# Seven-product tiles begin with a sum's product; the first block's product is copied from bank to bank and another accumulates onto it

## The chip, the core and the metric

The kernel runs on one core of one Trainium2 chip. The metric is the device time of one execution in microseconds (us); lower is better. A core has five engines that run side by side, each through its own instructions in order: TensorE (PE in the profile; its weight loads are PEld), VectorE (DVE), ScalarE (ACT), GpSimd (POOL) and SyncE (SP). They wait for each other by semaphores. Matrix products are written to PSUM, eight banks of 512 fp32 values in each of 128 partitions; everything else lies in SBUF.

## What is computed

One inference step of a small decoder of two layers, for 512 prompt tokens and 8 sample tokens together (520 columns), width 1024. Each layer is x += 0.5·SwiGLU(rms(x)), then a token mixer, then another 0.5·SwiGLU. So there are four SwiGLU blocks, and they are most of the work:

```python
def _swiglu(x, wg, wu, wd):
    return (jax.nn.silu(x @ wg) * (x @ wu)) @ wd      # 1024 -> 2816 -> 1024

for l in range(DEPTH):                                # DEPTH = 2
    x = x + 0.5 * _swiglu(_rmsnorm(x, norm_g[l, 0]), ...)
    x = x + mixer(_rmsnorm(x, norm_g[l, 1]))          # pooling in layer 0, attention in layer 1
    x = x + 0.5 * _swiglu(_rmsnorm(x, norm_g[l, 2]), ...)
```

Everything is fp32 to the reader. The kernel holds x transposed: a tile is 128 features by 520 tokens.

## The kernel before

**Products.** An fp32 matrix is held as a high and a low half (`xh`, `xl`; weights `wh`, `wl`), and a product is three passes: high·high, low·high, high·low. The halves of a weight piece of 128x512 are made on the chip: ACT rounds the raw piece to `wh` (L287), DVE subtracts to get `wl` (L288). Each piece so costs ACT one instruction and DVE one, and `_split` runs five pieces ahead of the product that uses them; `wh` and `wl` have six buffers each.

**Seven-product tiles.** A 2x2 block product needs eight block products; Strassen's scheme in Winograd's form needs seven, and more additions. Most tiles of the SwiGLU blocks are done so. For the up side (`strassen_tile`, 77 tiles) the two rows of the block matrix are the gate and the up weights of 128 hidden features, its two columns the two halves of the input features, and the token columns fall in two halves of 260. For the down side (`strassen_down`, 8 calls of 4 tiles, 32 tiles) the rows are two output tiles. The seven products are named by their weight piece and their moving side: A11·B11, S1·T1, S2·T2, A12·B21, S4·B22, S3·T3 and A22·T4. A11, A12, A22 are raw blocks; S1 is loaded by two DMAs that add up (`S` in the profile); S3 is a DMA that adds a block onto another; S2 (L221) and S4 (L227) are DVE additions in place on the raw piece. A product is 12 matmuls of 260 columns (L652; 4 slices of the contraction by 3 passes).

**Banks.** PSUM is handed out in pairs of banks, four pairs in all. A tile takes one bank `a` and a pair `c`. Before the change the up tile ran so: A11·B11 into `a`, copied by ACT to the first half of `sa` (L798); S1·T1 into the second bank of `c`, copied to `sb` (L803); then `finish()`, the last product A22·T4 of the tile before; S2·T2 onto `a`, copied to the second half of `sa` (L806); A12·B21 into the first bank of `c`; S4·B22 onto its second. DVE adds `sa` and both banks of `c` to `g` (L810, 520 columns), multiplies by `R`, the reciprocal norm of the tokens (L813), and ACT makes the Silu `t` (L814). S3·T3 goes onto `a`, DVE adds that to `sb` (L816) and multiplies by one half of `t` (L819), and the tile's last product A22·T4 onto `a` is multiplied by the other half (L821). The hidden tile `g` is then split into halves for the down side (L379, L380; and on the first two of a block's three parts the sums T1 to T4 of the down side are formed from a pair of such tiles by DVE, L709 to L729). The down tile is the same with L835, L837, L843 (copies), L850, L851 (add, multiply by `R`), L852, L854, L859 to L862. The first seven-product tile of each block (`early=True`, 4 in all) has its own order.

**What sets the order.** The program is recorded in this order, and a scheduler then orders the instructions of each engine; it may move a product's first matmuls ahead of another's. Weight pieces are listed in the order of the products (`sums`, `woven`): A11, S1, then A22 of the tile before, S2, A12, S4, S3. The ACT copies stand in ACT's one queue between the `wh` splits, so a copy comes after every split that the scheduler put ahead of it.

**Stages by time.** The SwiGLU blocks run at about 8 to 340, 380 to 710, 720 to 1050 and 1200 to 1500 us. Each is three parts: eight up tiles and a seven-product down side, the same again, then six up tiles and a plain down side.

Of the kernel before, what the change touches and what calls it, by code (L numbers as in the profile page):

```python
# [11 lines left out]
F32 = mybir.dt.float32  # L12
# [6 lines left out]
P = 128  # L19
# [120 lines left out]
class Weights:  # L140
# [99 lines left out]
    def sums(self, ch, again, first=False):  # L240

        v = self.combos(ch, again)
        head, rest = (("A11", "A12"), ("S4", "S1", "S2", "S3")) if first else (("A11", "S1"), ("S2", "A12", "S4", "S3"))
        for name in head:
            self.piece(ch, v[name])
        self.last()
        for name in rest:
            self.piece(ch, v[name])
        self.late = (ch, v["A22"])

    def woven(self, tiles):

        put = lambda i, *names: [self.piece(tiles[i][0], tiles[i][1][n]) for n in names]
        self.slow.add(tiles[1][0])
        put(0, "A11", "S1")
        self.last()
        put(1, "A11", "S1")
        put(0, "S2", "A12", "S4", "S3")
        put(1, "S2")
        put(0, "A22")  # L260
        put(1, "A12", "S4", "S3")
        for i in range(2, len(tiles)):
            put(i, "A11", "S1")
            put(i - 1, "A22")
            put(i, "S2", "A12", "S4", "S3")
        self.late = (tiles[-1][0], tiles[-1][1]["A22"])
# [58 lines left out]
def yoco_step(ctx, tc, ins, outs):  # L325
# [208 lines left out]
    def hcols(t, hf):  # L534
        return t[:, hf * H : (hf + 1) * H]


    def halves(t):
        return t.rearrange("p (h b a) -> p h b a", h=2, b=2)
# [5 lines left out]
    def back(z):  # L545

        return z.rearrange("p (b a) -> p b a", b=2)
# [9 lines left out]
    def out(bank):  # L557

        return bank[:, :H].rearrange("p (a b) -> p b a", b=2)
# [221 lines left out]
    def finish():  # L781
        if unfinished:
            unfinished.pop()()

    def strassen_tile(tmp, xx, tt, hs, early=False):

        B = lambda src, ks, hf: [tuple(hcols(z, hf) for z in src[k]) for k in ks]
        lo, up = range(4), range(4, 8)  # L790
        g = tmp.tile([P, TOK], F32, tag="g", name="g")
        t = tmp.tile([P, TOK], F32, tag="t", name="t")
        sa = tmp.tile([P, TOK], F32, tag="sa", name="sa")
        sb = tmp.tile([P, H], F32, tag="sb", name="sb", bufs=2)
        both, c = duo(), duo()
        a, b = both[:, 0, :], both[:, 1, :] if early else c[:, 1, :]
        product(B(xx, lo, 0), a)
        S.copy(back(hcols(sa, 0)), out(a))  # L798
        if early:
            product(B(xx, up, 0), c[:, 0, :])  # L800
            product(B(xx, up, 1), c[:, 1, :])
        product(B(tt, lo, 0), b)
        S.copy(back(sb), out(b))  # L803
        finish()
        product(B(tt, lo, 1), a, True)
        S.copy(back(hcols(sa, 1)), out(a))  # L806
        if not early:
            product(B(xx, up, 0), c[:, 0, :])
            product(B(xx, up, 1), c[:, 1, :], True)
        V.tensor_tensor(halves(g), halves(sa), outs(c), op=ALU.add)  # L810
        if early:
            V.tensor_tensor(hcols(g, 1), hcols(g, 1), sb, op=ALU.add)
        V.tensor_tensor(g, g, R, op=ALU.mult)  # L813
        S.activation(t, g, AF.Silu)  # L814
        product(B(tt, up, 0), a, True)
        V.tensor_tensor(back(sb), back(sb), out(a), op=ALU.add)  # L816

        def rest():
            V.tensor_tensor(hcols(g, 1), sb, hcols(t, 1), op=ALU.mult)  # L819
            product(B(tt, up, 1), a, True)  # L820
            V.tensor_tensor(back(hcols(g, 0)), out(a), back(hcols(t, 0)), op=ALU.mult)  # L821
            hidden(g, hs)

        unfinished.append(rest)

    def strassen_down(tmp, hs):
# [2 lines left out]

        def head(i):  # L830
            a, c = duo()[:, 0, :], duo()
            sa = tmp.tile([P, TOK], F32, tag="sa", name="sa")
            sb = tmp.tile([P, H], F32, tag="sb", name="sb", bufs=2)
            product(b["B11"], a)
            S.copy(back(hcols(sa, 0)), out(a))  # L835
            product(b["T1"], c[:, 1, :])
            S.copy(back(sb), out(c[:, 1, :]))  # L837
            st[i] = a, c, sa, sb

        def second(i):  # L840
            a, c, sa, sb = st[i]
            product(b["T2"], a, True)
            S.copy(back(hcols(sa, 1)), out(a))  # L843

        def third(i):
            a, c, sa, sb = st[i]
            product(b["B21"], c[:, 0, :])
            product(b["B22"], c[:, 1, :], True)
            u = tmp.tile([P, TOK], F32, tag="u", name="u", bufs=nu[0])
            V.tensor_tensor(halves(u), halves(sa), outs(c), op=ALU.add)  # L850
            V.tensor_tensor(u, u, R, op=ALU.mult)  # L851
            V.scalar_tensor_tensor(x[2 * i], u, -0.5, x[2 * i], op0=ALU.mult, op1=ALU.add)  # L852
            product(b["T3"], a, True)
            V.tensor_tensor(back(sb), back(sb), out(a), op=ALU.add)  # L854
# [1269 lines left out]
```

## Time and profile before

| | |
|---|---|
| median of 3 runs | 1534.68 us (1531.17 to 1536.09) |
| the profiled execution | 1533.06 us; its span, first to last instruction, 1531.3 us |
| mean granted TensorE clock | 0.998 |
| ACT busy | 968.8 us (63%) |
| POOL busy | 309.6 us (20%) |
| HBM | 147 GB/s over the span |

The profile is one execution. A group of instructions is a line of the kernel with an engine, an operation and operands; "mean ns of one" is its duration as recorded. Durations of following instructions overlap at their ends: 128x260 matmuls are recorded with 276 ns each, but start about 111 ns apart, and a DVE instruction of 128x520 is recorded with some 695 ns and the next starts about 0.61 us after it. So what an instruction takes from its engine is read from starts, and a busy share near 100% hides short waits. In a timeline row, what stands in brackets is the idle time before the instruction and what ended it.

### The profile page before, as it was taken

Reading aid. Unit: us, or ns where it says so; the run is one execution under the profiler, and the core shown is the slowest. Engines: PE = TensorE matmul, PEld = TensorE weight load, DVE = VectorE, ACT = ScalarE, POOL = GpSimd, SP = SyncE. Lnnn points to the kernel's source line nnn. Section 1 sums busy time; section 2 is a strip of 40 time slices with the busy share of each in tenths; the row PEclk is TensorE's granted clock in tenths of the full one; section 3 lists DMA queues with packets and bytes.
Section 4 is the critical chain, followed back from the end, with each engine's and each line's share of the span. In section 5 each row is a group of like instructions: output and inputs, shape, how many; then the busy total and the mean of one; then the engine's idle time right before and its main releaser. Section 6 shows DMA issues by size and latency. Waiting matters only on the chain. (4 is left out here: it accounts for less than half of the span.)

```text
span 1531.3 us, 35129 instructions
## 1 busy us (share of the span) xinstructions
PE 1507.3 (98%) x13338; PEld 1490.9 (97%) x13338; DVE 1407.0 (92%) x2799; ACT 968.8 (63%) x2030; POOL 309.6 (20%) x348
## 2 busy tenths in 40 slices
PE   9999999999999999999999999999999999999997
PEld 9999999999999999999999999999999999999997
DVE  6999999979999999989899999987887999999976
ACT  6765665657665665656665665655886765665555
POOL 1122222101122222100322221201561122222200
PEclk9999999999999999999999999999999999999999
DMA  9699889753688999845888998853434589988941
GB/s 244 125 192 199 188 190 203 179 173 119 139 195 183 196 193 193 179 127 131 202 191 188 198 196 184 185 173 87 88 69 99 124 180 191 197 191 189 205 130 57
DMA packets 420037, 255.43 MB, mean 167 GB/s; under 512 B 13182, under 2 KB 400246, under 8 KB 419828
## 3 DMA queue, kind: packets, MB, share of 16 engines
q1 hardware_dynamic: 339918, 187.56, 44.5%
q0 software_dynamic: 76192, 60.53, 28.2%
q10 hardware_dynamic: 3758, 5.09, 1.1%
q8 instruction: 105, 1.72, 0.5%
q14 instruction: 64, 0.52, 0.1%
HBM read 218.59 MB, written 6.11 MB: 147 GB/s over the span
## 5 line engine op out<-in xcount | busy, mean ns | idle before, releaser
L287 ACT ACTIVATE wh<-raw 128x512 fp32r<-128x512 f32 (+1 forms) x770 | 445.7, 616 | 242.6 <-DVE raw L221 79.5
L288 DVE TENSOR_TENSOR wl<-raw,wh 128x512 fp32r<-128x512 f32 (+1 forms) x770 | 501.5, 677 | 37.7 <-ACT wh L287 34.0
L652 PE MATMUL ps<-th,wh 128*128 128x260 f32 x1232 | 339.1, 276 | 0.6 <-ACT sb L803 0.4
L652 PE MATMUL ps<-th,wl 128*128 128x260 f32 x1232 | 337.7, 276 | 0.5 <-DVE wl L288 0.5
L652 PE MATMUL ps<-tl,wh 128*128 128x260 f32 x1232 | 338.1, 275 | 0.0
L652 PE MATMUL ps<-xh,wh 128*128 128x260 f32 x908 | 249.2, 276 | 1.2 <-ACT wh L287 0.9
L652 PE MATMUL ps<-xh,wl 128*128 128x260 f32 x908 | 248.7, 276 | 0.5 <-DVE wl L288 0.4
L652 PE MATMUL ps<-xl,wh 128*128 128x260 f32 x908 | 248.5, 276 | 0.0
L652 PEld LDWEIGHTS ps<-th,wh 128*128 128x128 f32 x1232 | 234.4, 190 | 2.0 <-ACT wh L287 0.9
L652 PEld LDWEIGHTS ps<-tl,wh 128*128 128x128 f32 x1232 | 234.5, 190 | 0.0
L652 PEld LDWEIGHTS ps<-th,wl 128*128 128x128 f32 x1232 | 233.6, 190 | 0.7 <-DVE wl L288 0.7
L398 POOL DMA_DIRECT2D S<-in_ffn_w_up_dram x77 | 102.1, 1326 | 419.4 <-DMA S<-in_ffn_w_up_dram 181.2
L652 PE MATMUL ps<-hh,wh 128*128 128x260 f32 x656 | 180.3, 278 | 3.5 <-ACT wh L287 1.7
L652 PE MATMUL ps<-hl,wh 128*128 128x260 f32 x656 | 179.4, 276 | 0.9 <-DVE hl L380 0.9
L652 PE MATMUL ps<-hh,wl 128*128 128x260 f32 x656 | 178.5, 275 | 0.0
L214 POOL DMA_DIRECT2D raw<-raw x109 | 96.1, 882 | 405.1 <-DVE wl L288 143.9
L652 PEld LDWEIGHTS ps<-xh,wh 128*128 128x128 f32 x908 | 172.4, 190 | 2.2 <-ACT wh L287 1.5
L652 PEld LDWEIGHTS ps<-xh,wl 128*128 128x128 f32 x908 | 172.2, 190 | 1.0 <-DVE wl L288 1.0
L652 PEld LDWEIGHTS ps<-xl,wh 128*128 128x128 f32 x908 | 172.5, 190 | 0.1
L652 PEld LDWEIGHTS ps<-hh,wh 128*128 128x128 f32 x656 | 124.2, 190 | 5.5 <-ACT wh L287 2.3
L652 PEld LDWEIGHTS ps<-hl,wh 128*128 128x128 f32 x656 | 124.4, 190 | 1.6 <-DVE hl L380 1.6
L652 PEld LDWEIGHTS ps<-hh,wl 128*128 128x128 f32 x656 | 124.1, 190 | 0.0
(370 smaller groups left out, 3609.5 us busy)
## 6 DMA issues: line engine op xcount, KB each, us to landing
raw<-in_ffn_w_gate_dram SPq DMA_DIRECT2D x87, 512.0 KB, 5.2
raw<-in_ffn_w_up_dram SPq DMA_DIRECT2D x87, 512.0 KB, 6.4
raw<-in_ffn_w_down_dram SPq DMA_DIRECT2D x128, 256.0 KB, 4.8
raw<-raw POOLq DMA_DIRECT2D x109, 256.0 KB, 4.2
S<-in_ffn_w_up_dram SPq DMA_DIRECT2D x77, 256.0 KB, 4.5
S<-in_ffn_w_up_dram POOLq DMA_DIRECT2D x77, 256.0 KB, 5.5
raw<-in_ffn_w_down_dram SPq DMA_DIRECT2D x16, 768.0 KB, 4.5
S<-in_ffn_w_down_dram SPq DMA_DIRECT2D x32, 256.0 KB, 3.1
```

Of the source, the lines that this page charges most:

```text
L214: G.dma_start(blk(raw, 2, 1), blk(raw, 1, 1), accum_op=ALU.add)
L287: pin(nc.scalar.activation(dh, src, AF.Copy))
L288: pin(nc.vector.tensor_tensor(dl, src, dh.bitcast(F32), op=ALU.subtract))
L398: return [ld(lambda t: t, a), lambda t: nc.gpsimd.dma_start(t, b, accum_op=ALU.add)]
L652: T.matmul(bank[:, :H], a[:, kk, :], two(b), start=(not more and kk == 0 and i == 0), stop=(kk == 3 and i == 2), skip_group_check=more,)
```

## The change

The seven-product tiles that aren't `early`, on the up and the down side, begin with S1·T1 and then do A11·B11; the weight pieces are listed in that order. The copy of A11·B11 goes from bank `a` into the first bank of `c` instead of into `sa`, as the whole bank's 260 columns in their order; A12·B21 then accumulates onto it (`more=True`). Only the copy of `a` after S2·T2 still goes to `sa`, which needs 260 columns. DVE adds that copy to the second bank of `c`, in place in PSUM (260 columns), and multiplies both banks by `R` in one instruction of 520 columns that reads PSUM. The number of products, matmuls, copies, splits and DMAs is the same.

```diff
     def sums(self, ch, again, first=False):
-        head, rest = (("A11", "A12"), ("S4", "S1", "S2", "S3")) if first else (("A11", "S1"), ("S2", "A12", "S4", "S3"))
+        head, rest = (("A11", "A12"), ("S4", "S1", "S2", "S3")) if first else (("S1", "A11"), ("S2", "A12", "S4", "S3"))
...
     def woven(self, tiles):
-        put(0, "A11", "S1")
+        put(0, "S1", "A11")
...
         for i in range(2, len(tiles)):
-            put(i, "A11", "S1")
+            put(i, "S1", "A11")
...
     def strassen_tile(tmp, xx, tt, hs, early=False):
-        product(B(xx, lo, 0), a)
-        S.copy(back(hcols(sa, 0)), out(a))
         if early:
+            product(B(xx, lo, 0), a)
+            S.copy(back(hcols(sa, 0)), out(a))
             product(B(xx, up, 0), c[:, 0, :])
             product(B(xx, up, 1), c[:, 1, :])
         product(B(tt, lo, 0), b)
         S.copy(back(sb), out(b))
+        if not early:
+            product(B(xx, lo, 0), a)
+            S.copy(c[:, 0, :H], a[:, :H])
         finish()
         product(B(tt, lo, 1), a, True)
-        S.copy(back(hcols(sa, 1)), out(a))
-        if not early:
-            product(B(xx, up, 0), c[:, 0, :])
+        if early:
+            S.copy(back(hcols(sa, 1)), out(a))
+            V.tensor_tensor(halves(g), halves(sa), outs(c), op=ALU.add)
+            V.tensor_tensor(hcols(g, 1), hcols(g, 1), sb, op=ALU.add)
+            V.tensor_tensor(g, g, R, op=ALU.mult)
+        else:
+            S.copy(hcols(sa, 1), a[:, :H])
+            product(B(xx, up, 0), c[:, 0, :], True)
             product(B(xx, up, 1), c[:, 1, :], True)
-        V.tensor_tensor(halves(g), halves(sa), outs(c), op=ALU.add)
-        if early:
-            V.tensor_tensor(hcols(g, 1), hcols(g, 1), sb, op=ALU.add)
-        V.tensor_tensor(g, g, R, op=ALU.mult)
+            V.tensor_tensor(c[:, 1, :H], hcols(sa, 1), c[:, 1, :H], op=ALU.add)
+            V.tensor_tensor(halves(g), outs(c), halves(R), op=ALU.mult)
         S.activation(t, g, AF.Silu)
...
     def strassen_down(tmp, hs):
         def head(i):
-            product(b["B11"], a)
-            S.copy(back(hcols(sa, 0)), out(a))
             product(b["T1"], c[:, 1, :])
             S.copy(back(sb), out(c[:, 1, :]))
+            product(b["B11"], a)
+            S.copy(c[:, 0, :H], a[:, :H])
         def second(i):
             product(b["T2"], a, True)
-            S.copy(back(hcols(sa, 1)), out(a))
+            S.copy(sa, a[:, :H])
         def third(i):
-            product(b["B21"], c[:, 0, :])
+            product(b["B21"], c[:, 0, :], True)
             product(b["B22"], c[:, 1, :], True)
-            V.tensor_tensor(halves(u), halves(sa), outs(c), op=ALU.add)
-            V.tensor_tensor(u, u, R, op=ALU.mult)
+            V.tensor_tensor(c[:, 1, :H], sa, c[:, 1, :H], op=ALU.add)
+            V.tensor_tensor(halves(u), outs(c), halves(R), op=ALU.mult)
```

The scheduler makes another order of it. Three places show what it moved; line numbers are those of each kernel, and the numbers in the names of raw pieces and banks are the same in both.

**ACT, a regular up tile** (the third part of a block; `ps_14278` is its bank `a`, `ps_14279` the second bank's pair `c`, `raw_13964` its weights, `raw_14101` and `S` those of the next tile). Before:

```order
L803 COPY sb<-ps_14279 128x260 [waits PE_49]
L287 ACTIVATE wh<-raw_13964 128x512 [waits DVE_49,Activation_49]
L287 ACTIVATE wh<-raw_13964 128x512 [waits DMAHW0_49,DMASW0_49]
L287 ACTIVATE wh<-raw_14101 128x512 [waits DMAHW2_49,Activation_49]
L287 ACTIVATE wh<-S 128x512 [waits DMASW1_49,PE_49,Activation_49]
L806 COPY sa<-ps_14278 128x260 [waits PE_49]
```

And now:

```order
L803 COPY sb<-ps_14279 128x260 [waits PE_49]
L287 ACTIVATE wh<-raw_13964 128x512 [waits DVE_49,Activation_49]
L287 ACTIVATE wh<-raw_13964 128x512 [waits DMAHW0_49,DMASW0_49,Activation_49]
L287 ACTIVATE wh<-S 128x512 [waits DMASW1_49,PE_49,Activation_49]
L806 COPY ps_14279<-ps_14278 128x260 [waits PE_49,Activation_49]
L287 ACTIVATE wh<-raw_14101 128x512 [waits DMAHW2_49,PE_49]
```

The split that waits for DVE is that of S4. Before, the copy of A11·B11 (L798) stood ahead of the first row; now it is the fifth row, behind the splits of S4, S3 and the next tile's S1, the last of which also waits for PE.

**PE, the third tile of a down side** (third block, second part; `ps_14000` is its bank `a`, `ps_13711` and `ps_13783` are the banks `a` of the first and second tile). Before, where S2·T2 (`ps_14000<-xh`) begins:

```order
L652 MATMUL ps_13711<-ph,wl 128x260
L652 MATMUL ps_13711<-ph,wh 128x260
L652 MATMUL ps_13711<-pl,wh 128x260
L652 MATMUL ps_13711<-ph,wl 128x260
L652 MATMUL ps_14000<-xh,wh 128x260
L652 MATMUL ps_14000<-xl,wh 128x260
```

And now:

```order
L652 MATMUL ps_14000<-hl,wh 128x260
L652 MATMUL ps_14000<-hh,wl 128x260
L652 MATMUL ps_13783<-ph,wh 128x260
L652 MATMUL ps_13783<-pl,wh 128x260
L652 MATMUL ps_13783<-ph,wl 128x260
L652 MATMUL ps_14138<-xh,wh 128x260
L652 MATMUL ps_14138<-xl,wh 128x260
L652 MATMUL ps_14000<-xh,wh 128x260
L652 MATMUL ps_14000<-xl,wh 128x260
```

Before, the twelve matmuls of a whole other product (`ps_13711<-ph`) stood between the end of A11·B11 (`ps_14000<-hh,wl`) and S2·T2, and the product S1·T1 behind them. Now five matmuls stand between.

**PE, the start of the same down side** (`ps_13571` is bank `a` of the last up tile, whose last product ends in the first row; `ps_13711`, `ps_13712` are `a` and `c` of the first down tile, `ps_13783`, `ps_13784` of the second). Before, from the ninth matmul of S2·T2 on, then A12·B21's first, then the second tile's S1·T1:

```order
L652 MATMUL ps_13711<-xh,wl 128x260
L652 MATMUL ps_13712<-xh,wh 128x260
L652 MATMUL ps_13784<-xh,wh 128x260
L652 MATMUL ps_13784<-xl,wh 128x260
L652 MATMUL ps_13784<-xh,wl 128x260
```

And now, from near the end of the first nine matmuls of A12·B21:

```order
L652 MATMUL ps_13712<-xl,wh 128x260
L652 MATMUL ps_13712<-xh,wl 128x260
L652 MATMUL ps_13783<-hh,wh 128x260
L652 MATMUL ps_13783<-hl,wh 128x260
L652 MATMUL ps_13783<-hh,wl 128x260
```

S1·T1 of the second tile now stands ahead of the last up tile's last product, and A11·B11 of the second tile (`ps_13783<-hh`) takes the place behind eighteen matmuls of the first down tile. The orders of SP's and POOL's DMAs are the same in both kernels, row by row.

More of the change, by code (lines that the diff above doesn't have):

```diff
@@ L254, in woven @@
         self.slow.add(tiles[1][0])
-        put(0, "A11", "S1")
+        put(0, "S1", "A11")
         self.last()
-        put(1, "A11", "S1")
+        put(1, "S1", "A11")
         put(0, "S2", "A12", "S4", "S3")
@@ L831, in head @@
             a, c = duo()[:, 0, :], duo()
-            sa = tmp.tile([P, TOK], F32, tag="sa", name="sa")
+            sa = tmp.tile([P, TOK], F32, tag="sa", name="sa")[:, :H]
             sb = tmp.tile([P, H], F32, tag="sb", name="sb", bufs=2)
-            product(b["B11"], a)
-            S.copy(back(hcols(sa, 0)), out(a))
             product(b["T1"], c[:, 1, :])
             S.copy(back(sb), out(c[:, 1, :]))
+            product(b["B11"], a)
+            S.copy(c[:, 0, :H], a[:, :H])
             st[i] = a, c, sa, sb
```

## The prediction, made before the changed kernel was run

> **What bounds the kernel.** I read the page's table of engines first, then stretches of time, then PE's waits.
>
> ```profile
> PE 1507.3 (98%) x13338; PEld 1490.9 (97%) x13338; DVE 1407.0 (92%) x2799; ACT 968.8 (63%) x2030; POOL 309.6 (20%) x348
> ```
>
> PE is the bound, and DVE stands close behind. How much PE has left is read from counts, since its busy share hides short waits. The next view gives four stretches with nearly all seven-product tiles, and one that is full (columns: stretch, then busy us and instructions of PE, PEld, DVE, ACT, POOL, then clock and DMA):
>
> ```profile
> 60.00:300.00 240.00, 238.20 (x2109) 236.20 (x2107) 233.94 (x436) 147.77 (x304) 52.48 (x48) 1.00 0.91 194
> 410.00:600.00 190.00, 188.19 (x1661) 186.47 (x1661) 186.35 (x349) 117.56 (x242) 41.50 (x38) 1.00 0.87 186
> 740.00:950.00 210.00, 208.55 (x1847) 206.95 (x1847) 203.18 (x380) 129.79 (x266) 47.36 (x45) 1.00 0.87 186
> 1215.00:1430.00 215.00, 212.21 (x1875) 210.14 (x1875) 210.37 (x396) 132.69 (x272) 46.98 (x44) 1.00 0.87 185
> 600.00:700.00 100.00, 100.00 (x898) 100.00 (x897) 90.79 (x160) 61.85 (x119) 10.94 (x10) 1.00 0.69 166
> ```
>
> The full stretch has 898 matmuls in 100 us, 0.1114 us each, at full clock. The four others have 7492 in 855 us, which would take 834.3 us. So 20.7 us of PE's time is lost there, 1.3% of the run: no edit that leaves the matmuls alone can win more. DVE is busy 833.85 of the 855 us, 97.5%: in these stretches it is nearly a second bound.
>
> Which waits are they? The waits of the seven-product matmuls' line (us, times):
>
> ```profile
> its engine sat idle before it (us, times) until:
>   ACT wh L287: 2.6, 3
>   DVE wl L288: 1.0, 2
>   DVE hl L380: 0.9, 2
>   DVE g L821: 0.8, 3
>   ACT sa L843: 0.7, 3
>   ACT hh L379: 0.5, 1
>   ACT sb L803: 0.4, 1
>   DVE g L810: 0.4, 1
>   ACT sa L835: 0.3, 1
> ```
>
> That is 7.6 us in 17 waits. Each costs more than its row says, as starts show, here where a down side begins in the fourth block:
>
> ```profile
> 1276.98 0.28 PE L652 MATMUL ps<-hh,wh 128*128 128x260 f32 x1
> 1277.53 0.38 PE L652 MATMUL ps<-hh,wh 128*128 128x260 f32 x1 [0.28 <-DVE g L821]
> 1277.75 0.28 PE L652 MATMUL ps<-hl,wh 128*128 128x260 f32 x1
> ...
> 1279.09 0.28 PE L652 MATMUL ps<-hh,wl 128*128 128x260 f32 x1
> 1280.23 0.38 PE L652 MATMUL ps<-hh,wh 128*128 128x260 f32 x1 [0.87 <-ACT wh L287]
> ```
>
> From 1276.98 to 1277.53 is 0.55 us, 0.44 more than the usual 0.11, where the row says 0.28; and the next start comes after 0.22, another 0.11. So a wait costs its row and 0.27 us: 7.6 + 17·0.27 = 12.2 us. The rest of the 20.7 us is waits too short for a row.
>
> **The second wait of that piece** is DVE's doing, through ACT:
>
> ```profile
> 1277.51 0.64 ACT L379 ACTIVATE hh<-g 128x520 fp32r<-128x520 f32 x1 [0.86 <-DVE g L821]
> 1278.51 1.67 ACT L287 ACTIVATE wh<-raw 128x512 fp32r<-128x512 f32 x3 [0.36 <-DVE raw L227]
> 1280.09 0.35 ACT L837 COPY sb<-ps 128x260 f32<-128x260 f32 x1
> ```
>
> ACT waited 0.86 us for the last up tile's multiply on DVE (L821), then for S4's addition (L227), and then made three splits, the third of which PE waited for. An ACT split takes (1280.09 − 1278.51)/3 = 0.53 us.
>
> **What the change takes from DVE.** Groups by shape, then starts:
>
> ```profile
> L813 DVE TENSOR_TENSOR g<-g,R 128x520 f32<-128x520 f32 x77 | 53.6, 696 | 0.0
> L810 DVE TENSOR_TENSOR g<-sa,ps 128x520 f32<-128x520 f32 x77 | 53.3, 692 | 1.1 <-PE ps L652 0.8
> L821 DVE TENSOR_TENSOR g<-ps,t 128x260 f32<-128x260 f32 x77 | 32.6, 424 | 6.6 <-PE ps L652 6.5
> L930 DVE TENSOR_TENSOR u<-ps,R 128x520 f32<-128x520 f32 x29 | 20.1, 696 | 6.4 <-PE ps L624 6.4
> L720 DVE TENSOR_TENSOR t<-g 128x260 f32<-128x260 f32 x32 | 13.7, 427 | 0.4
> ```
>
> ```profile
> 1346.59 0.43 DVE L819 TENSOR_TENSOR g<-sb,t 128x260 f32<-128x260 f32 x1
> 1346.93 0.43 DVE L821 TENSOR_TENSOR g<-ps,t 128x260 f32<-128x260 f32 x1
> 1347.27 0.69 DVE L288 TENSOR_TENSOR wl<-raw,wh 128x512 fp32r<-128x512 f32 x1
> 1347.87 0.69 DVE L810 TENSOR_TENSOR g<-sa,ps 128x520 f32<-128x520 f32 x1
> 1348.47 1.29 DVE L288 TENSOR_TENSOR wl<-raw,wh 128x512 fp32r<-128x512 f32 x2
> ```
>
> A tile loses an addition of 520 (692 ns) and a multiply (696), and gets an addition of 260 (424, as L821) and a multiply that reads PSUM (696, as L930): 0.268 us less, and the same from starts (0.60 against 0.34). With 73 up tiles and 32 down tiles that is 105·0.268 = 28.1 us of DVE: its share of the four stretches falls to 94.2%. No row has DVE or ACT writing PSUM. For DVE's addition the ends are 424 and 692 ns, so the relief lies between 28 us and nothing; I take 424, the row of the same width with a PSUM operand. For ACT's copy to a bank I take the 0.36 us of its copies to SBUF (the L837 row), between nothing and one split's 0.53.
>
> The Trainium skill ("Perfetto Trace Analysis", Optimizing Scalar/DVE Operations) speaks against this: it gives DVE a fixed cost of some 60 ns an instruction on SBUF and 125 on PSUM. By it, an estimate: the 260-wide addition and the multiply would both pay the higher cost where now one of two does, 65 ns a tile, and the relief would be 21 us. The rows above do not bear it out for reads: L821 reads PSUM and L720 does not, and they take 424 and 427 ns.
>
> Relief that PE doesn't wait for is worth nothing, so I count waits. By the order shown, at the start of a down side the second tile's S1·T1 no longer stands behind the last up tile's multiply (3 waits on L821), A11·B11 of the second tile fills PE while ACT makes the splits (3 on `wh`), and 28 instead of 14 matmuls lie between S2·T2 and S3·T3 of the first tile, which hides its copy (3 on L843). These nine cost 2.6 + 0.8 + 0.7 + 9·0.27 = 6.5 us. Of the other eight (3.5 + 8·0.27 = 5.7 us) I let a third go with DVE's backlog: 1.9 us. **Gain 8.4 us**; ends 1.6 (the copy waits alone, 0.7 + 3·0.27) and 12.2.
>
> **What it adds: a nearer wait.** S2·T2 may not start before the copy of A11·B11 has read `a`. Between them lay two products; now it is one, or less. Behind the copy in ACT's queue stand the splits that follow, and behind S2·T2 all of PE. When can the copy start?
>
> ```profile
> 1349.69 0.28 PE L652 MATMUL ps<-xh,wl 128*128 128x260 f32 x1
> 1350.00 0.38 ACT L798 COPY sa<-ps 128x260 f32<-128x260 f32 x1 [1.75 <-PE ps L652]
> ```
>
> 0.31 us after the product's last matmul starts. But ahead of it now stands the split of the next S1, which waits until PE has read A11's buffer: 0.31 + 0.53 + 0.36 = 1.20 us after that start. In most tiles 12 to 16 matmuls lie between, so S2·T2 is due at 13·0.111 = 1.45 us or later: covered, with 0.25 to 0.6 us to spare, and each 0.1 us that ACT is later than that costs up to 95·0.1 us. In the third tile of seven down sides, and in three early up tiles, only 2 to 5 matmuls lie between; with five, PE is ready at 6·0.111 = 0.67 us and waits 0.53. The split needs only the eleventh matmul, so up to 0.11 us less: I take 0.45. **Ten such tiles cost 4.5 us**; ends 0, if ACT finds the split done, and 10, if one more split (0.53) is ahead.
>
> The S1 piece is wanted one product (1.34 us) earlier. Its loads keep their places in SP's and POOL's queues. Now ACT waits for them little:
>
> ```profile
> ACT wh L287 <- DMA S<-in_ffn_w_down_dram: 2.5, 5, 1.0
> ```
>
> I cost it at nothing, because pieces are split five products ahead of use; without that cover it would be 1.34 us more at these five, 6.7 us.
>
> **Sum.** 1533.06 (the profiled execution, span and 1.8 us around it) − 8.4 + 4.5 = 1529.2 us. The median of the runs lies 1.6 us higher, so on its scale 1530.8; I say **1530**.
>
> **Rivals.**
>
> *ACT comes late to the copy in many tiles (slower).* The first of the splits ahead of the copy is that of S4, which waits for DVE's addition L227:
>
> ```profile
> ACT wh L287 <- DVE raw L227: 50.4, 52, 2.9
> ```
>
> That is 0.97 us in each of 52 waits. Before, PE didn't feel it, because pieces are five ahead; now the copy stands behind. From the end of S1·T1 to S2·T2 are 26 matmuls, 2.9 us, and three splits and the copy take 1.95: if the split of S4 begins more than 0.9 us after S1·T1 ends, PE waits. If DVE were as late as now, 52 tiles would pay 0.97 less the spare (some 0.36) less the relief of a tile (0.27), 0.34 us: 17.7 us, **1547**. For it speaks DVE's share of 97.5%; against it that DVE, 28 us lighter, can catch up, and that a wait of PE gives it more time, so that the lateness isn't paid in each tile anew.
>
> *The relief is hidden anyway.* The waits at a down side's start may be the length of the last tile's chain (multiply, split, subtract), not a backlog. Then only the copy waits go: 1533.06 − 1.6 + 4.5 = **1536**. For it: PE is full in the middle of the parts. Against it: the order puts other matmuls there.
>
> *All named waits go and none come*: 1533.06 − 12.2 = **1521**. It needs ACT at the ten near tiles in time.
>
> **How the numbers follow.** The forecast has 0.50, late copies 0.20, hidden 0.18, all go 0.12. About 0.3% (4.6 us) is what a measurement here tells from no change, so faster means under 1530.1: the forecast lies at that edge and, since its gain has more room than its cost, gives 0.30 to faster, 0.18 to the same and 0.02 to slower. With 0.12 from all-go, faster is 0.42; with 0.18 from hidden, the same is 0.36; with the late copies, slower is 0.22. The range goes from 1519, below all-go, to 1545, which takes in both ends of the ten tiles' cost and half of the late copies.
>
> **What would show it.** DVE's busy time near 1379 us with the addition near 424 ns and the multiply near 696; the copy to a bank near 0.36 us; no wait of PE on L821's successor at three starts of down sides; new waits of PE on the copy to a bank, some 0.2 to 0.3 us by their rows, in ten tiles. The forecast is wrong if PE's row for that copy is tens of waits long, if DVE's addition takes near 692 ns, or if 7492 matmuls fill the same 855 us as before.

## The result, and the profile after

The changed kernel takes 1538.26 us (median of 12 runs, 1534.63 to 1541.59), the kernel before 1532.24 us beside it (12 runs, 1530.12 to 1536.09). The ratio is 1.0037, with a 95% interval of 1.0026 to 1.0048: some 6 us slower, where 2 us less was forecast. The profiled execution took 1536.96 us, 3.9 us more than that of before.

The engines' line of the page of the changed kernel:

```profile
PE 1506.1 (98%) x13338; PEld 1491.1 (97%) x13338; DVE 1390.0 (91%) x2799; ACT 985.3 (64%) x2030; POOL 310.2 (20%) x348
```

DVE is busy 17.0 us less, and PE has as many matmuls. ACT's 16.5 us more are no more work: added up from the trace, the durations of its 2030 instructions make 1100.6 us before and 1100.9 us after, but fewer of them follow each other so closely that they overlap (1229 instead of 1391). The same four stretches as in the prediction (columns: stretch, then busy us and instructions of PE, PEld, DVE, ACT, POOL, clock and DMA):

```profile
60.00:300.00 240.00, 236.62 (x2093) 234.59 (x2093) 229.35 (x433) 151.14 (x301) 52.47 (x48) 1.00 0.89 193
410.00:600.00 190.00, 187.00 (x1654) 185.47 (x1653) 183.84 (x355) 122.39 (x246) 41.51 (x38) 1.00 0.87 185
740.00:950.00 210.00, 208.28 (x1846) 206.79 (x1845) 198.22 (x379) 130.72 (x264) 50.96 (x52) 1.00 0.88 189
1215.00:1430.00 215.00, 212.48 (x1882) 211.11 (x1883) 208.23 (x401) 138.20 (x277) 46.97 (x44) 1.00 0.86 182
```

They hold 7475 matmuls where they held 7492: reckoned as in the prediction (100/898 us each), 22.6 us are lost instead of 20.7. DVE's share went from 97.5% to 819.64/855 = 95.9%, and PE got nothing for it. What PE waits for, in the seven-product matmuls' line:

```profile
  ACT wh L287: 5.0, 10
  ACT sb L803: 3.0, 3
  DVE g L819: 1.1, 2
  DVE sb L822: 0.4, 1
  DVE xl L380: 0.3, 1
```

The waits at the starts of the down sides (on L821, now L827, and on L843, now L849) have gone; others have come. I added up, from the starts of all matmuls of these stretches, what each start lies beyond 0.111 us. Before, 18.8 us are lost in gaps worth naming, 15.5 of them around the starts of down sides. After, it is 19.8 us, only about 2 of them there. The rest is new, in three groups:

- the third tile of all eight down sides, 0.71 us each: 5.8 us
- two up tiles in the second part of each block, 0.36 us each: 2.9 us
- the first seven-product tiles of blocks 1, 2 and 4: 8.6 us (2.5 before)

The first group, in PE's timeline (start us, us, engine, line, operation):

```profile
236.03 0.28 PE L652 MATMUL ps<-xh,wl 128*128 128x260 f32 x1
236.14 0.28 PE L652 MATMUL ps<-ph,wh 128*128 128x260 f32 x1
236.25 0.28 PE L652 MATMUL ps<-pl,wh 128*128 128x260 f32 x1
236.36 0.28 PE L652 MATMUL ps<-ph,wl 128*128 128x260 f32 x1
237.08 0.38 PE L652 MATMUL ps<-hh,wh 128*128 128x260 f32 x1 [0.44 <-ACT wh L287]
237.29 0.28 PE L652 MATMUL ps<-hl,wh 128*128 128x260 f32 x1
237.40 0.32 PE L652 MATMUL ps<-hh,wh 128*128 128x260 f32 x1
```

A11·B11 ends in the first row, and S2·T2 begins in the last. Between them stand the last three matmuls of the tile before (`ph`) and the first two of the next tile's S1·T1, which wait for their split. ACT at that time:

```profile
235.35 1.15 ACT L287 ACTIVATE wh<-raw 128x512 fp32r<-128x512 f32 x2 [0.98 <-DVE raw L227]
236.41 0.61 ACT L287 ACTIVATE wh<-S 128x512 fp32r<-128x512 f32 x1
236.93 0.36 ACT L843 COPY ps<-ps 128x260 f32<-128x260 f32 x1
```

ACT waited 0.98 us for the addition of S4 on DVE, made the splits of S4, S3 and S1 one behind the other, and only then the copy to the bank, 0.9 us after A11·B11's last matmul had begun. What PE's row names is the split of S1, which ends at 237.02; the copy ends at 237.29, 0.11 us before S2·T2 starts. Both stand in one queue behind the same two splits, and PE has only the rest of one product with which to fill the time. The second group is the same thing in an up tile, here with twelve matmuls between:

```profile
177.41 1.15 ACT L287 ACTIVATE wh<-raw 128x512 fp32r<-128x512 f32 x2 [0.65 <-DVE raw L227]
178.47 0.61 ACT L287 ACTIVATE wh<-S 128x512 fp32r<-128x512 f32 x1
178.99 0.37 ACT L806 COPY ps<-ps 128x260 f32<-128x260 f32 x1
```

```profile
178.76 0.28 PE L652 MATMUL ps<-th,wl 128*128 128x260 f32 x1
179.13 0.38 PE L652 MATMUL ps<-th,wh 128*128 128x260 f32 x1
179.35 0.28 PE L652 MATMUL ps<-tl,wh 128*128 128x260 f32 x1
179.46 0.33 PE L652 MATMUL ps<-th,wh 128*128 128x260 f32 x1
```

From 178.76 to 179.13 are 0.26 us too many, and 0.10 more follow: 0.36 us, in a gap too short for a row among the waits. One up tile earlier, also with twelve matmuls between, no split stands ahead of the copy: it begins 0.37 us after the start of the product's last matmul (168.04), and PE has no gap:

```profile
168.41 0.36 ACT L806 COPY ps<-ps 128x260 f32<-128x260 f32 x1 [0.29 <-PE ps L652]
168.68 1.15 ACT L287 ACTIVATE wh<-raw 128x512 fp32r<-128x512 f32 x2
```

So in these sixteen tiles it is the place in ACT's queue, behind the split that waits for DVE, that decides.

A further loss stands outside these stretches: between the 2640th and the 3120th matmul (305.8 to 361.4 us before), where the pool block follows the first block, the changed kernel falls back by 3.9 us. PE's waits in the whole run have this row, and ACT's from 300 to 352 us the two below it:

```profile
PE pv L580 <- DVE acc L996: 2.9, 1, 2.9
```

```profile
ACT G L1182 <- DMA pr<-in_bands_dram: 4.8, 1, 4.8
ACT th L379 <- DMA pr<-in_pool_w_dram: 3.2, 1, 3.2
```

The kernel before has there `ACT G L1176 <- DMA pr<-in_bands_dram: 3.0, 2, 1.8` and 2.0 us for the second: ACT reaches these loads later, waits longer for them, hands its splits to DVE later, and DVE's sums are then late for PE.

The wait is only a part of the 3.9 us. Behind it the granted clock is halved for 3.41 us (the column behind POOL), where the kernel before has 1.00 from 345 to 360 us:

```profile
353.10:356.50 3.40, 3.40 (x19) 3.40 (x18) 2.75 (x11) 1.75 (x5) 0.00 (x0) 0.50 0.00 0
```

Half of 3.41 us is 1.7 us, so by this estimate 2.2 us are the wait and 1.7 us the clock. Over the 12 runs of the changed kernel the mean granted clock is 0.996, in the nine runs of the kernel before beside the next experiment 0.998. These 0.002 of 1538 us, an estimate too, make about 3 of the 6 us by which the changed kernel is slower.

### The profile page after: what moved, and what is told of

Read it like the earlier page. It is cut to its first block, busy times and chain, and to the rows that moved or that the text cites. A ratio compares the mean times of both kernels' runs of the same rounds, so it can differ in the third digit from the quotient of the medians.

```text
span 1535.1 us, 35134 instructions
## 1 busy us (share of the span) xinstructions
PE 1506.1 (98%) x13338; PEld 1491.1 (97%) x13338; DVE 1390.0 (91%) x2799; ACT 985.3 (64%) x2030; POOL 310.2 (20%) x348
## 3 DMA queue, kind: packets, MB, share of 16 engines
q0 software_dynamic: 76192, 60.53, 28.1%
## 5 line engine op out<-in xcount | busy, mean ns | idle before, releaser
L287 ACT ACTIVATE wh<-raw 128x512 fp32r<-128x512 f32 (+1 forms) x770 | 458.5, 618 | 270.8 <-PE ps L652 130.9
L288 DVE TENSOR_TENSOR wl<-raw,wh 128x512 fp32r<-128x512 f32 (+1 forms) x770 | 509.6, 674 | 60.9 <-ACT wh L287 56.9
L652 PE MATMUL ps<-th,wh 128*128 128x260 f32 x1232 | 336.9, 277 | 6.2 <-ACT sb L803 3.0
L652 PE MATMUL ps<-th,wl 128*128 128x260 f32 x1232 | 336.5, 275 | 0.0
L652 PE MATMUL ps<-tl,wh 128*128 128x260 f32 x1232 | 336.0, 275 | 0.0
L652 PE MATMUL ps<-xh,wh 128*128 128x260 f32 x908 | 250.0, 276 | 1.5 <-ACT wh L287 1.3
L652 PE MATMUL ps<-xl,wh 128*128 128x260 f32 x908 | 249.9, 275 | 0.4 <-DVE xl L380 0.3
L652 PE MATMUL ps<-xh,wl 128*128 128x260 f32 x908 | 249.3, 275 | 0.0
L652 PEld LDWEIGHTS ps<-th,wh 128*128 128x128 f32 x1232 | 232.9, 190 | 9.9 <-ACT sb L803 3.6
L652 PEld LDWEIGHTS ps<-tl,wh 128*128 128x128 f32 x1232 | 234.1, 190 | 0.0
L652 PEld LDWEIGHTS ps<-th,wl 128*128 128x128 f32 x1232 | 233.3, 190 | 0.0
L652 PE MATMUL ps<-hh,wh 128*128 128x260 f32 x656 | 180.0, 276 | 2.8 <-ACT wh L287 2.8
L652 PE MATMUL ps<-hl,wh 128*128 128x260 f32 x656 | 180.8, 276 | 0.1
L652 PE MATMUL ps<-hh,wl 128*128 128x260 f32 x656 | 179.4, 275 | 0.0
L652 PEld LDWEIGHTS ps<-xh,wh 128*128 128x128 f32 x908 | 172.3, 190 | 2.6 <-ACT wh L287 2.1
L652 PEld LDWEIGHTS ps<-xl,wh 128*128 128x128 f32 x908 | 172.5, 190 | 0.8 <-DVE xl L380 0.8
L652 PEld LDWEIGHTS ps<-xh,wl 128*128 128x128 f32 x908 | 172.4, 190 | 0.0
L652 PEld LDWEIGHTS ps<-hh,wh 128*128 128x128 f32 x656 | 124.1, 190 | 3.9 <-ACT wh L287 3.9
L652 PEld LDWEIGHTS ps<-hl,wh 128*128 128x128 f32 x656 | 124.6, 190 | 0.5 <-DVE hl L380 0.3
L652 PEld LDWEIGHTS ps<-hh,wl 128*128 128x128 f32 x656 | 124.2, 190 | 0.0
```

What stands on the lines that cost most here:

```text
L287: pin(nc.scalar.activation(dh, src, AF.Copy))
L288: pin(nc.vector.tensor_tensor(dl, src, dh.bitcast(F32), op=ALU.subtract))
L652: T.matmul(bank[:, :H], a[:, kk, :], two(b), start=(not more and kk == 0 and i == 0), stop=(kk == 3 and i == 2), skip_group_check=more,)
```

## The experiments

The theory with which I went in (A in the expectations): the copy to the bank, waited for by S2·T2, costs more than DVE's lighter load and the new order of the matmuls gain. Its rivals: the gain comes from the order alone; the splits are late whatever the copy does; the loss at the pool block is chance. All ratios are against the kernel before, on the same chip, with 95% intervals.

**The changed kernel once more** (`again`, no edit).

> The changed kernel once more, nothing edited. Theory A (the waits in the seven-product stretches cost 1.1 us net, the 3.9 us around 343 to 352 us at the end of the first block are lost each time): near 1537 to 1539 us, and the trace shows again PE idle for about 3 us between the pool block's products (L1221) and the sums of L580, with ACT waiting some 5 us for the bands' load. Theory B (that gap is chance, from DMAs that happen to collide): the same time, but the gap is under 1.5 us in this trace and the loss stands elsewhere.

1537.55 us, ratio 1.0033 (1.0021 to 1.0046). The gap at the pool block is there again (`PE pv L580 <- DVE acc L996: 2.9, 1, 2.9`; one of ACT's waits for the bands' load 4.7 us), and from the 2640th to the 3120th matmul 5.4 us are lost: the wait is as long, but the clock is at 0.50 from 350.0 to 356.8 us, twice as long as in the first trace. So the wait is no chance of one execution; how long the clock is halved behind it differs.

**Only the order** (`order_only`).

```diff
-            S.copy(c[:, 0, :H], a[:, :H])
+            S.copy(back(hcols(sa, 0)), out(a))
...
-            product(B(xx, up, 0), c[:, 0, :], True)
+            product(B(xx, up, 0), c[:, 0, :])
...
-            V.tensor_tensor(c[:, 1, :H], hcols(sa, 1), c[:, 1, :H], op=ALU.add)
-            V.tensor_tensor(halves(g), outs(c), halves(R), op=ALU.mult)
+            V.tensor_tensor(halves(g), halves(sa), outs(c), op=ALU.add)
+            V.tensor_tensor(g, g, R, op=ALU.mult)
```

(the same in the down sides)

> Only the order of the products and pieces is changed (S1 times T1 first); A11 times B11 is copied to SBUF as before and DVE adds 520 wide. Theory A (the order buys the nearer wait, DVE's lighter load buys most of the gain at the starts of the down sides): the 16.6 us of waits on the splits and copies stay or grow, the gain shrinks from 13 to about 5 us: 1541 to 1548 us, slower than the changed kernel. Rival (the gain at the down sides comes from the other order of the matmuls, not from DVE): like the changed kernel, 1536 to 1540 us.

1546.85 us, 1.0093 (1.0079 to 1.0107). As theory A had it: with DVE's old load the near copy (now to SBUF) costs more. No matmul accumulates onto a copied bank here, so the loss does not need that. Its waits:

```profile
PE ps L652 <- ACT wh L287: 5.6, 6, 1.0
PE ps L652 <- ACT sa L843: 3.0, 4, 0.9
...
PE ps L652 <- ACT sa L806: 2.6, 10, 0.5
```

**Only the arithmetic** (`relief_only`), A11·B11 first as before, copied to the bank:

```diff
-            product(b["T1"], c[:, 1, :])
-            S.copy(back(sb), out(c[:, 1, :]))
             product(b["B11"], a)
             S.copy(c[:, 0, :H], a[:, :H])
+            product(b["T1"], c[:, 1, :])
+            S.copy(back(sb), out(c[:, 1, :]))
```

(the same in the up tiles, and the pieces A11, S1 in the old order)

> Only the arithmetic is changed: A11 times B11 first as before, but copied to the bank, with A12 times B21 accumulated onto it and the narrow addition on DVE. Theory A: none of the new waits (eight at the third down tile, eight at up tiles with 12 matmuls between, some 8 us at the first seven-product tiles of a block), and about 8 of the 13 us gained: 1523 to 1528 us, faster than both. Rival (DVE's relief is worth nothing because the waits at the down sides are the length of a chain): 1530 to 1534 us, the same as before, with DVE busy some 17 us less.

1553.37 us, 1.0133 (1.0117 to 1.0148): a miss for both. The timeline shows why; PE first, then ACT:

```profile
130.26 0.28 PE L652 MATMUL ps<-xh,wl 128*128 128x260 f32 x1
130.98 0.38 PE L652 MATMUL ps<-hh,wh 128*128 128x260 f32 x1 [0.45 <-ACT ps L841]
```

```profile
130.57 0.36 ACT L841 COPY ps<-ps 128x260 f32<-128x260 f32 x1 [0.86 <-PE ps L652]
```

S1·T1 goes to the other bank of the pair to which the copy writes, and the program makes it wait for the copy, with nothing between: 0.71 us in this tile. PE has 28 such waits by their rows, 16 in the down sides (6.8 us) and 12 in the up tiles (6.0 us). So this was no test of DVE's relief, but it shows what a tile avoids that begins with S1·T1.

**Up tiles in the old order, down sides as changed** (`mix_up_down`; the edit above in the up tiles alone).

> Up tiles as in the kernel before in order, with the bank copy and the narrow addition; down sides in full as in the changed kernel. Theory A: the waits of the up tiles go (8.0 us at the first tiles of blocks, 2.9 at the eight tiles with 12 matmuls between), the eight waits at the third down tile stay (5.7 us), the gain at the down sides' starts of about 13 us stays: 1524 to 1529 us, under the changed kernel by some 10 us. Rival (the up tiles' order has no part): 1536 to 1540 us.

1549.11 us, 1.0109 (1.0095 to 1.0123). The same miss, in the up tiles: `PE ps L652 <- ACT ps L804` has 5.9 us in 13 waits.

**DVE's relief alone** (`relief_free`), without any copy to a bank. The kernel before, with the narrow addition and the multiply from PSUM; the share of A11·B11 in the first half is left out.

```diff
             product(B(xx, up, 0), c[:, 0, :])
             product(B(xx, up, 1), c[:, 1, :], True)
-        V.tensor_tensor(halves(g), halves(sa), outs(c), op=ALU.add)
-        V.tensor_tensor(g, g, R, op=ALU.mult)
+            V.tensor_tensor(c[:, 1, :H], hcols(sa, 1), c[:, 1, :H], op=ALU.add)
+            V.tensor_tensor(halves(g), outs(c), halves(R), op=ALU.mult)
```

> The kernel before in order, with the narrow addition into the bank and the multiply from it, but A12 times B21 begins its bank afresh, so that no copy to a bank and no wait on one exists; the share of A11 times B11 in the first half is left out. It is DVE's relief (0.27 us in each of 105 tiles) and nothing else. Theory A (most of the gain of 13 us at the down sides' starts is DVE's backlog): 1521 to 1526 us. Rival (that gain is the other order of the matmuls): 1530 to 1534 us with DVE's busy time near 1379 to 1390 us all the same.

1528.72 us, 0.9973 (0.9963 to 0.9984). Between the two: with the old order the relief is worth 4.1 us.

**The changed kernel without the copy** (`no_copy`).

```diff
             product(B(xx, lo, 0), a)
-            S.copy(c[:, 0, :H], a[:, :H])
...
-            product(B(xx, up, 0), c[:, 0, :], True)
+            product(B(xx, up, 0), c[:, 0, :])
```

(the same in the down sides)

> The changed kernel without the copy to the bank: S2 times T2 follows A11 times B11 with no copy between, A12 times B21 begins its bank afresh, and the share of A11 times B11 in the first half is left out. Theory A (the copy, waited for by S2 times T2, is what the new waits come from): the eight waits of 0.36 us, the eight of 0.71 at the third down tile and about half of the 8 us at the first tiles go: 1524 to 1528 us. Rival (the splits are late, the one of S4 behind DVE's addition L227 above all, and PE would wait for a split in the same places): 1533 to 1538 us, with the waits on wh still 4 us or more by their row.

1521.75 us, 0.9937 (0.9925 to 0.9949), 11 us under the kernel before and 16 under the changed one. That is theory A, and more than it asked. The splits' row keeps 3.7 us in 5 waits, not far from the 4 us that the rival asked for, but not in the same places: 1.7 us of it is one wait that ends at 455.6 us, behind which the clock is at 0.50 from 456.9 to 460.3 us. The profiled execution is the slowest of the six (1526.69 us).

**A copy for which nobody waits** (`copy_unwaited`). As the last, with this in the copy's place:

```diff
+            S.copy(hcols(sa, 0), R[:, :H])
```

> As no_copy (the share of A11 times B11 in the first half left out), but ScalarE makes a copy of the same width from SBUF to SBUF at the copy's place in the program, for which nobody waits. Theory A (it is PE's wait for the copy that costs, not ScalarE's 37 us of time): 1521 to 1525 us, like no_copy. Rival (ScalarE's time delays the splits): half of the 16 us or more come back, 1529 us or more.

1518.64 us, 0.9912 (0.9899 to 0.9925). ACT's busy time is back (967.8 us, against 935.6 without a copy) and costs PE nothing. The copy even holds up ACT's queue: ACT is idle 68.8 us in all ahead of these copies, for the most part until DVE has done its addition, which reads `sa`. So it is not what ACT does that costs, but that PE has to wait for it. PE's waits in the seven-product line, and the four stretches:

```profile
  ACT wh L287: 0.8, 3
  DVE wl L288: 0.6, 2
  DVE g L819: 0.3, 1
```

```profile
60.00:300.00 240.00, 239.40 (x2139) 238.87 (x2138) 231.56 (x442) 151.94 (x311) 52.46 (x48) 1.00 0.91 195
410.00:600.00 190.00, 188.94 (x1677) 187.89 (x1678) 182.97 (x350) 118.27 (x244) 43.71 (x40) 1.00 0.90 193
740.00:950.00 210.00, 210.00 (x1883) 210.00 (x1882) 203.34 (x388) 131.09 (x270) 47.23 (x43) 1.00 0.89 193
1215.00:1430.00 215.00, 214.93 (x1917) 214.28 (x1916) 208.41 (x399) 133.81 (x275) 51.61 (x47) 1.00 0.91 196
```

7616 matmuls: only 6.9 us of the 855 are lost. With the kernel before it is 20.7, and the mean granted clock of the runs is 0.998, as there. The 3 us between this run and the last are not settled; the order that the scheduler makes differs in the two. In this kernel A12·B21 does not accumulate onto a copy either; whether that costs anything is read from `copy_ahead` below.

**Down sides as changed, up tiles as before** (`down_only`).

```diff
-            product(B(xx, lo, 0), a)
-            S.copy(c[:, 0, :H], a[:, :H])
+            S.copy(back(hcols(sa, 0)), out(a))
```

(in the up tiles, with the old order, addition and multiply there)

> Down sides as in the changed kernel, up tiles' products and arithmetic as in the kernel before, except that S1 times T1 still comes after A11 times B11 there. Theory A (down sides gain some 13 us at their starts by their own order and pay 5.7 us at the third tile; the up tiles only cost): 1524 to 1528 us, under both kernels. Rival (the gain at the down sides' starts needs the lighter load of the up tiles before them): 1532 to 1538 us.

1557.71 us, 1.0167 (1.0154 to 1.018), far beyond both expectations:

```profile
PE ps L652 <- ACT ps L843: 16.9, 8, 2.9
```

One wait in each down side, 2.1 us on average: the copy stands in ACT's queue behind the splits of the last up tiles' results, and those (in the second down side at 221.03 us, after 1.46 us of waiting) behind DVE's multiply L827. With the up tiles' old load DVE is later, and the near copy passes that on to PE. Behind three of these waits (2.4 us each) the clock is halved for 3.41 us, from 225.9, 471.7 and 1301.1 us, an estimate of 1.7 us each; behind the others it is not.

**The tiles ahead of the pool block as before** (`tail_as_before`): the six up tiles of the first block's third part take the old order and arithmetic.

```diff
-                    strassen_tile(tmp, mov, tt, hs, j == NPL[fi])
+                    strassen_tile(tmp, mov, tt, hs, j == NPL[fi], (fi, pi) == (0, 2))
```

> The changed kernel, but the six up tiles of the first block's third part, ahead of the pool block, are as in the kernel before. Theory A (the 4 us lost at 343 to 352 us come from ScalarE's order at the end of these tiles, which makes it wait 5 us for one load of the bands): 1533 to 1535 us, PE's gap ahead of the sums of L580 gone or near 1 us. Rival (the gap comes from how the loads collide, whatever these tiles do): 1536.5 to 1538.5 us with a gap near 3 us.

1536.25 us, 1.0026 (1.0017 to 1.0035). From the 2640th to the 3120th matmul 1.3 us are lost instead of 3.9, and the wait has moved to another place (`PE pv L1226 <- DVE u L941`, 2.2 us once). The median lies between the expectations. Most of what is gained in that place is the clock, which is not halved behind this wait; the wait itself is 0.7 us shorter by its row. So these tiles have a part in that wait, but a small one.

**The copy ahead of the splits** (`copy_ahead`), complete arithmetic:

```diff
-            S.copy(c[:, 0, :H], a[:, :H])
+            later(S.copy(c[:, 0, :H], a[:, :H]))
+            W.pin = later
+            W.prefetch()
+            W.pin = lambda ins: ins
```

(S1·T1 and A11·B11 no longer call `W.prefetch()` themselves; `later` keeps the order of the program)

> The changed kernel, complete, but the copy to the bank stands ahead of the three splits (S4, S3 and the next S1) in ScalarE's queue, which are issued and kept in order behind it. Theory A (the copy is late because it stands behind the split of S4, which waits for DVE's addition): the waits of 0.36 and 0.71 us at sixteen tiles and some of the 8 us at the first tiles go, while a wait on a later split may come: 1522 to 1529 us, faster than both kernels. Rival (the nearness itself costs: with 12 matmuls between, or because the splits are then late): 1533 to 1540 us.

1534.2 us, 1.0019 (1.0009 to 1.0028). ACT's timeline at the place of the third tile shown above:

```profile
234.68 0.36 ACT L847 COPY ps<-ps 128x260 f32<-128x260 f32 x1 [1.02 <-PE ps L653]
236.41 1.15 ACT L287 ACTIVATE wh<-raw 128x512 fp32r<-128x512 f32 x2 [1.38 <-DVE raw L227]
```

The copy is now made as soon as the product ends, and ACT's wait for S4's addition comes behind it. The gaps of 0.71 and 0.36 us at the sixteen tiles are gone, and so is the loss at the pool block (0.1 us gained there, with the clock at 1.00). But only 4 of the 16 to 19 us come back, and the time is the rival's:

```profile
PE ps L653 <- ACT sb L804: 3.0, 3, 1.0
PE ps L653 <- DVE g L823: 2.9, 5, 0.8
PE ps L653 <- ACT ps L807: 2.0, 4, 0.5
```

The first tiles of three blocks wait nearly as they did, and at the starts of down sides PE waits for DVE again. In six down sides 0.57 us more goes in gaps too short for a row: in the second of them PE starts late at 460.24 and at 460.76 us, each time 0.05 us after the end of a split (L287) that the edit has put behind the copy. So theory A holds for the sixteen tiles, and the rival for these: with the copy ahead the splits are late. The copy's place among these three splits alone wins 4 us and no more.

The same run shows that an accumulation onto a copied bank costs nothing by itself. Ten such copies are made in this stretch, and it has 896 matmuls in 100 us, where the full stretch of the prediction has 898:

```profile
466.00:566.00 100.00, 100.00 (x896) 100.00 (x895) 97.43 (x185) 61.30 (x127) 22.62 (x21) 1.00 0.90 193
```

**The bank copy written behind S1·T1** (`late_copy`), A11·B11 first, complete arithmetic:

```diff
-            product(b["T1"], c[:, 1, :])
-            S.copy(back(sb), out(c[:, 1, :]))
             product(b["B11"], a)
+            product(b["T1"], c[:, 1, :])
             S.copy(c[:, 0, :H], a[:, :H])
+            S.copy(back(sb), out(c[:, 1, :]))
```

> A11 times B11 first, S1 times T1 second, as before the change, and the copy to the bank is written in the program behind S1 times T1, so that this product does not wait for it as in relief_only; complete arithmetic. Theory A (relief_only was slow only because S1 times T1, the first to write the same pair of banks, waited for the copy): 1526 to 1531 us, like relief_free. Rival (an accumulation onto a copied bank costs by itself): 1535 us or more.

1538.7 us, 1.0043 (1.0031 to 1.0055). S1·T1 no longer waits for the copy, yet the time is that of the changed kernel: PE waits 8.1 us in 22 waits for splits (L287) and 1.9 us in two for the copy. The time is the rival's, but not its reason, since the full stretch of `copy_ahead` accumulates onto copied banks too; which of the waits comes first here was not followed further.

**The copy ahead, and the second and third seven-product tiles of each block as before** (`copy_ahead_first_old`).

```diff
+OLD = lambda j, n: 0 < j - n < 3
...
-                    strassen_tile(tmp, mov, tt, hs, j == NPL[fi])
+                    strassen_tile(tmp, mov, tt, hs, j == NPL[fi], OLD(j, NPL[fi]))
```

> As copy_ahead, and the second and third seven-product tiles of each block are as in the kernel before; complete arithmetic. Theory A (the waits of 0.8 to 1.3 us in the first tiles of three blocks, 8 waits, come from the new order there): they go and the old waits of these places (2.5 us in all) come back: 1527 to 1531 us, under the kernel before. Rival (they come from how ScalarE and DVE are filled there by the last plain tile, whichever order the products have): 1533 to 1536 us.

1533.91 us, 1.0015 (1.0006 to 1.0024). The time is the rival's. The gap at 67 us went from 1.27 to 0.81 us, and those at 82 and 91 us went away, as theory A had it; but around the first down side of the first block its profiled execution (1539.24 us, the slowest of eleven) loses 5 us more than that of `copy_ahead`. Two gaps of 1.3 and 1.9 us stand there, and behind the second the clock is at 0.50 from 108.7 to 112.1 us, an estimate of 1.7 us. What makes these gaps was not followed further, and with a profile of the slowest execution the run settles little. No complete version was faster than the kernel before.

## Why the prediction was wrong, by its own steps

**The bound was right.** PE had some 20 us to win in the four stretches: `copy_unwaited` is 13.6 us faster, and its stretches are full to 6.9 us. A wait costs its row and 0.27 us: at 236.36 us the row says 0.44, and the two starts behind it come 0.61 and 0.10 late, 0.71 in all.

**DVE's relief was sized right by durations, to the tenth of a us.** Groups by shape after (the early tile of each block keeps the old form):

```profile
L819 DVE TENSOR_TENSOR g<-ps,R 128x520 f32<-128x520 f32 x73 | 50.6, 694 | 1.0
L818 DVE TENSOR_TENSOR ps<-sa,ps 128x260 f32<-128x260 f32 x73 | 31.2, 428 | 4.1 <-PE ps L652 1.4
L857 DVE TENSOR_TENSOR u<-ps,R 128x520 f32<-128x520 f32 x32 | 22.2, 693 | 0.3
L856 DVE TENSOR_TENSOR ps<-sa,ps 128x260 f32<-128x260 f32 x32 | 13.7, 427 | 0.0
L806 ACT COPY ps<-ps 128x260 f32<-128x260 f32 x73 | 26.8, 367 | 4.5 <-PE ps L652 3.3
```

The addition into the bank takes 428 ns (424 taken), the multiply 694 (696), the copy 367 (0.36 us). With 5.5 us for the four early tiles these groups have 123.2 us; those they replace had 53.6 + 53.3 on the up side and, in L850 and L851, 22.1 + 22.3 us: 28.1 us less. DVE's busy total fell by 17.0 us only, to 1390.0 us and not to 1379, since its instructions overlap when they follow closely (0.34 us from start to start at 0.43 of duration), and now fewer do (2300 instead of 2426). Of DVE's share in the four stretches the prediction took off all 28 us; only 82 of the 105 tiles make their multiply in them, so it should have been 95.0%, and 95.9% was measured. By the Trainium skill ("Perfetto Trace Analysis", Optimizing Scalar/DVE Operations), whose dearer PSUM access would have made it 21 us (an estimate from its 60 and 125 ns), the addition into PSUM would be some 65 ns slower than one on SBUF alone; at 428 and 421 ns (L825, all SBUF) it is 7 ns slower, and the trace does not agree.

**The gain was sized too low: 8.4 us forecast, 13.6 measured** (1532.27 − 1518.64, all waits on the copy away). The nine waits at three down sides went, as said. Of the other eight I let go a third, and of the 8.5 us in waits too short for a row nothing; in all, 13.8 of the 20.7 us went. DVE's relief alone gives 4.1 us with the old order. That the other 9.5 us are the new order's is the difference only: no run has the new order alone without its wait. (The lower end of the gain, 0.7 + 3·0.27, is 1.5 us and not 1.6, and the rivals' times stand 1.6 us lower than the forecast, which alone was moved to the scale of the median; neither changes a choice.)

**The step that failed is the nearer wait: "Ten such tiles cost 4.5 us".** With the wait the ratio is 1.0037, without it 0.9912: 1.3%, some 19 us. So the cost was sized 15 us too low and the gain 5 us too low; that the sum (3.9 us gained, where 6.0 were lost) is off by 10 us and no more is luck, since the two errors have opposite signs. The step went wrong in three places.

- It took the split of S1 alone to stand ahead of the copy (0.31 + 0.53 + 0.36 = 1.20 us). In the third tiles that came out nearly so, 1.26 us from the start of A11·B11's last matmul to the copy's end at 237.29; but there are eight, and each pays 0.71, not 0.45, since I had counted the row and not the 0.27 behind it: 5.8 us for 3.2. The 1.26 us is in part luck: the split of S1 began at 236.41 not because PE still held A11's buffer, but because the splits of S4 and S3 ended then, which had waited for DVE. And the rows of these waits name that split, not the copy to the bank, as the prediction had expected.
- It called tiles with 12 to 16 matmuls between covered. Those with 14 and 16 were, since no gap shows in them. Eight of those with 12 were not, because there all three splits stand ahead and the first waits for L227: 2.9 us, where the prediction has nothing. That is the mechanism of the first rival ("ACT comes late to the copy"), which I priced in 52 tiles and gave 0.20; it holds in sixteen places and more. The Trainium skill says of ScalarE's queue ("TensorE: Matmul & The Clock Gate", the table ahead of What a matmul computes) that it is strictly first in, first out; the copy at 236.93 us, whose product had been over since 236.31, agrees.
- It priced three early up tiles at 0.45 us each. The tiles behind a block's plain tiles pay 8.6 us: there the copy of S1·T1 too stands behind splits (in the first block behind two that begin at 66.89 us, after 1.52 us of waiting), and PE waits for it (`ACT sb L803: 3.0, 3`) and for a split. Some of that isn't the near copy's: `copy_unwaited` still loses 1.1 us in the first tiles of block 1 and as much in block 2.

**Outside the four stretches I had looked at nothing**, and 3.9 us were lost there, behind the first block, 1.7 of them by the halved clock. It is the same queue: with the copy ahead of the splits this loss is gone, and without the wait too. The four losses make 5.8 + 2.9 + 8.6 + 3.9 = 21.2 us; less the 2.2 us that remain without the wait, that is the 19 us.

**The earlier S1 piece costs nothing, as I had it**, though ACT waits for its load more (11.3 us in 8 waits after, 2.5 in 5 before): in `copy_unwaited` it does so just as long (10.7 us in 7), and PE doesn't.

## What to carry to other kernels

When an edit moves a wait nearer to the bound engine, don't price it from the two instructions alone: walk up the queue of the engine that must serve it, take every row that stands ahead, and ask of each what it waits for; here one split that waits for another engine held up a copy that had all it needed. A wait that costs nothing behind five products' lead becomes the bound when the lead is one product. And test such a wait by running the kernel without it: the copy's time cost nothing, and that PE had to wait for it some 19 us, of which its place behind three splits was 4.

## What the runs showed that I had not expected

- 105 copies on ACT cost nothing (1518.64 us with copies that nobody waits for, 1521.75 without them), and the same number with PE waiting for them cost some 19 us.
- Two products into the two banks of one pair are not free of each other in this program: after a copy to one bank the product into the other waited for it in `relief_only`, with 28 waits by their rows.
- Half of a change can be far worse than all of it: the changed down sides with the old up tiles took 1557.71 us, 19 us more than both together, since the near copy hands DVE's lateness on to PE.
- A long wait of PE can cost more than itself. Behind the one of 2.9 us at the pool block the clock was halved for 3.41 us in the changed kernel and for 6.8 us in `again`; behind one of 2.2 us in `tail_as_before` it was not.
